# Ordering the weight differences, the residual's turns and its moves between the splits of a decoder layer

## The chip, the cores and the metric

The kernel runs on one core of a Trainium2 chip. A core has five engines that take their instructions in order, each from its own queue: TensorE (PE; its weight loads are listed apart as PEld), VectorE (DVE), ScalarE (ACT), GpSimd (POOL) and SyncE (SP, which here only starts transfers). Sixteen DMA engines carry the transfers. The metric is the device time of one execution in microseconds (us).

## What is computed

One decoder layer over 272 tokens (16 meta tokens and 256 others) of width 2048, all in float32: an attention and pooling mixer, a first layer norm, and a gated feed-forward block with a short convolution, followed by a second layer norm. The change lies in the feed-forward block, of which the reference is

```python
def conv_gated_ffn(h, w_up, conv_w, conv_b, w_down):
    T = h.shape[1]
    z = h @ w_up
    zp = jnp.pad(z, ((0, 0), (CONV_WIDTH - 1, 0), (0, 0)))
    z = sum(zp[:, j:j + T] * conv_w[j] for j in range(CONV_WIDTH)) + conv_b
    a, g = jnp.split(z, 2, axis=-1)
    return (jax.nn.gelu(a) * g) @ w_down
...
    h = layer_norm(ALPHA * h + mix, ln1_g[l], ln1_b[l])
    f = conv_gated_ffn(h, w_up[l], conv_w[l], conv_b[l], w_down[l])
    h = layer_norm(ALPHA * h + f, ln2_g[l], ln2_b[l])
```

`w_up` is 2048 x 11264 (an `a` half and a `g` half of 5632 columns each), `w_down` 5632 x 2048.

## The kernel before

*Weights as a stream.* All weights come as blocks of 128 partitions x 2048 float32 (1 MB) in one fixed order, the list `stream`. A block is landed in a raw tile `wraw`, of which there are three, by a transfer that SyncE starts (L111). It is then split into two float32r parts of less precision, `whl`: ScalarE copies the upper part (L124), VectorE subtracts it from the raw block to get the lower part (L125), in two pieces of 128x1024. A product is then three matmuls: weight upper by activation upper, upper by lower, and lower by upper. A raw tile is free for the transfer three blocks on when its split has been read from it. `weights()` hands out the next block and has blocks up to two further ones recorded ahead of it.

*The feed-forward plan.* The 44 column groups f of the `a` and `g` halves are taken in six parts of 8, 8, 8, 8, 8 and 4 groups (`PARTS`). An *up* item multiplies a block of `w_up` for one f and one half (48 matmuls, L196 to L198, into a PSUM tile `mm`, of which there are four), and its result goes through the convolution `conv` (ScalarE at L715, VectorE at L716 and L717). After the second half `gate` applies the GELU (ACT, L732) and the product (DVE, L733). From the second part on each up item is followed by a *down* item for the part in front, in the function `seven`: it multiplies 256 x 256 x 1024 by seven products in place of eight (Strassen's scheme in Winograd's form). Its A items use four, its B items three of the products (L780 to L782, PSUM tiles `at`). The scheme needs sums and differences of the operands. For the gated activations `forms` makes them on GpSimd (L752 to L755) and splits them (L738 on ACT, L739 on DVE). For the weights they are made in place in the raw tile by VectorE, in `fetch`: one difference in an A block (L116), three operations in a B block (L119 to L121), all 128x512, ahead of the block's split. At the end of four A or B items their products are added to the result `y2` (L788, L792 to L807).

*The residual's way.* The layer's input to the feed-forward block, `y`, lies with channels on the partitions, and `y2` must hold it with tokens on the partitions. It is turned within 32x32 squares by VectorE (L871, one transposition for each of 16 channel groups), and 32 DMA transfers on ScalarE's queue (`residual`, L709; the list `moves`) then carry the squares to their places in `y2`. The part of a move that i numbers is the half of the tokens; all moves of the first half come first.

*What sets the order.* The code is traced, and a scheduler then decides the order in which each engine's instructions stand; they are run in that order. Within `with tc.issue_after(ins)` every instruction traced on the engine of `ins` is ordered behind `ins`. It adds no wait between engines. `behind(i)` uses it with the last upper and the last lower split of block i, which `fetch` returns. The number of the next block to be used is `state["use"]`.

In the up items from f = 4 (`FOLDED`) on, the loop's last lines count them by b = 2 (f - FOLDED) + half. Behind the splits of the next block to be used it records four turns for each b below 4 and, from b = 4 on, four moves, until none is left. These lines stand after the product and its convolution. The first down item comes after b = 8.

Of the kernel before, what the change touches and what calls it, by code (L numbers as in the profile page):

```python
# [14 lines left out]
ALU = mybir.AluOpType  # L15
# [4 lines left out]
NM = 16  # L20
# [4 lines left out]
KT = D // P  # L25
# [11 lines left out]
FOLDED = 4  # L37
# [31 lines left out]
def tile_layer(ctx, tc, xt, w_first, w_proj, w_uk, w_uv, w_pool, w_o, w_up, w_down, cols, rows, rel_bias, onehot, out):  # L69
    nc = tc.nc  # L70
# [7 lines left out]
    def big():  # L78
        return pm.tile([P, 512], F32, tag="mm", name="mm")
# [12 lines left out]
    stream = [w_proj[j] for j in range(8)] + [w_uk, w_uv] + [w_proj[j] for j in range(8, 24)]  # L92
    stream += [w_o[j] for j in range(KT)]
    plan = ffn_plan()
    kinds = {}
# [11 lines left out]
    ready, raws, split = {}, {}, {}  # L107
    state = {"next": 0, "use": 0}

    def fetch(raw, hl, src, kind=None):  # L110
        nc.sync.dma_start(raw, src)  # L111
        b11, b12, b21, b22 = (raw[:, c:c + 512] for c in range(0, 2048, 512))
        cuts = (0, 1024, 2048)
        if kind == "A":

            nc.vector.tensor_tensor(b12, b12, b11, op=ALU.subtract)  # L116
        if kind == "B":

            nc.vector.tensor_tensor(b12, b22, b12, op=ALU.subtract)  # L119
            nc.vector.tensor_tensor(b11, b12, b11, op=ALU.add)  # L120
            nc.vector.tensor_tensor(b21, b21, b11, op=ALU.subtract)  # L121
            cuts = (0, 1024, 1536)
        for c in (slice(a, b) for a, b in zip(cuts, cuts[1:])):
            upper = nc.scalar.activation(hl[:, 0, c], raw[:, c], AF.Copy)  # L124
            lower = nc.vector.tensor_tensor(hl[:, 1, c], raw[:, c], hl[:, 0, c].bitcast(F32), op=ALU.subtract)  # L125
        return upper, lower

    def weight_tiles():
        raw = wp.tile([P, 2048], F32, tag="wraw", name="wraw")
        return raw, wp.tile([P, 2, 2048 + 2], F32R, tag="whl", name="whl")  # L130

    def emit(i):
        if i in ready:
            return
        if i == last:

            raw = wp.tile([P, 2048], F32, tag="wraw", name="wraw")
            nc.sync.dma_start(raw, stream[i])
            raws[i] = raw
            ready[i] = []  # L140
            for c in range(0, 2048, 256):
                hl = ring.tile([P, 2, 258], F32R, tag="act", name="whl_r", padded_shape=[P, 2, T])
                nc.scalar.activation(hl[:, 0, :256], raw[:, c:c + 256], AF.Copy)
                nc.vector.tensor_tensor(hl[:, 1, :256], raw[:, c:c + 256], hl[:, 0, :256].bitcast(F32), op=ALU.subtract)
                ready[i].append(hl)
            return
        if i == spare:
            raw = wp.tile([P, 2048], F32, tag="wraw", name="wraw")
            hl = sb.tile([P, 2, 2048 + 2], F32R, tag="y", name="whl_y")
        else:  # L150
            raw, hl = weight_tiles()
        split[i] = fetch(raw, hl, stream[i], kinds.get(i))
        ready[i] = hl
        if i >= spare:
            raws[i] = raw
# [6 lines left out]
    def weights(ahead=2):  # L162
        i = state["use"]
        state["use"] += 1
        prefetch(i + 1 + ahead)
        return ready.pop(i)

    @contextmanager
    def behind(i):

        upper, lower = (getattr(ins, "ins", ins) for ins in split[i])
        with tc.issue_after(upper), tc.issue_after(lower):
            yield

# [7 lines left out]
    def row_sums(i, hl):  # L182

        total = sb.tile([P, 1], F32, name=f"total{i}")
        nc.scalar.activation(raws[i], raws[i], AF.Copy, accum_out=total)
        hi, lo = (hl[-1][:, p, 256:] if isinstance(hl, list) else hl[:, p, 2048:] for p in range(2))
        nc.scalar.activation(hi, total.to_broadcast([P, 2]), AF.Copy)
        nc.vector.tensor_tensor(lo, total.to_broadcast([P, 2]), hi.bitcast(F32), op=ALU.subtract)
# [16 lines left out]
    for k0, k1 in [(k, k + 1) for k in range(9)] + [(9, 12), (12, 15), (15, 16)]:  # L205
        if k0 == KT - 1:

            raw = ap_.tile([P, 1024], F32, name="wraw_l", tag="v1")[:, :T + MF].rearrange("p (a b) -> p a b", a=1)
        elif k0 % 3 == 0:
            raw = wp.tile([P, 2048], F32, tag="wraw", name="wraw")  # L210
            raw = raw[:, :3 * (T + MF)].rearrange("p (a b) -> p a b", b=T + MF)
        if k0 % 6 == 0:
            hl = wp.tile([P, 2, 2048 + 2], F32R, tag="whl", name="whl")
# [60 lines left out]
    for i in range(2):  # L274
        nc.vector.tensor_tensor(kidx[DI * i:DI * i + DI, 1 + i, :], ps[:DI, :T], kidx[:DI, 0, :].bitcast(F32),
                                op=ALU.subtract)
# [89 lines left out]
    for j in range(8):  # L366
        hl = weights()
# [34 lines left out]
    y = sb.tile([P, KT, T], F32, tag="y", name="x", padded_shape=[P, KT, T])  # L402
# [37 lines left out]
    src = score  # L440
    for r in range(TOPK // 8):
# [4 lines left out]
        src = work  # L446
# [6 lines left out]
    for h in range(H):  # L453
        hl = weights()
# [127 lines left out]
    for h in range(H):  # L582
# [3 lines left out]
        hl = weights()  # L586
# [118 lines left out]
    def residual(a, b, i):  # L705

        src, dst, t = slice(32 * a, 32 * a + 32), slice(32 * b, 32 * b + 32), NM + i * P + 32 * b
        to = y2[dst, i, :].rearrange("p (m d) -> p m d", d=P)[:, :, src]
        nc.scalar.dma_start(to, y[src, :, t:t + 32])  # L709

    moves = [(a, b, i) for i in range(2) for a in range(4) for b in range(4)]

    def conv(j, half_, src, za):
# [98 lines left out]
    for item in plan:  # L812
        if item[0] in "AB":
            seven(*item)
            continue
        if item[0] == "down":
            _, part, c, g = item
            hl = weights()
            if c == 1:
                emit((last, spare)[g])  # L820
                if g == 0:
                    row_sums(last, ready[last])
            if g == 0:
                downs = [big(), big()]
            n = PARTS[part]
            for k in range(4 * g, 4 * g + 4):
                w = slice(512 * (k - 4 * g), 512 * (k - 4 * g) + 512)
                for i in range(2):
                    a, r = pairs[part][k // 2][f"a{i + 1}{k % 2 + 1}"]
                    nc.tensor.matmul(downs[i], a[:, 0, r], hl[:, 0, w], start=k == 0, stop=False)  # L830
                    nc.tensor.matmul(downs[i], a[:, 0, r], hl[:, 1, w], start=False, stop=False)  # L831
                    nc.tensor.matmul(downs[i], a[:, 1, r], hl[:, 0, w], start=False, stop=k == n - 1)  # L832
            if g == n // 4 - 1:
                for i in range(2):
                    yc = y2[:, i, 512 * c:512 * c + 512]
                    nc.vector.tensor_tensor(yc, yc, downs[i], op=ALU.add)
            continue
        _, f, half_ = item
        part = next(p for p in range(len(PARTS)) if f < sum(PARTS[:p + 1]))
        if half_ == 0:  # L840
            if f % 2 == 0:
                pair = fp.tile([P, 2, S], F32, name="za", tag="z0", bufs=3)
            both = []
        hl = weights()
        ps = big()
        if todo and f > FOLDED + half_:
            p, r = todo.pop(0)
            with behind(state["use"]):
                pairs[p].append(forms(r, len(pairs[p]), p == FAST))
        if f < FOLDED:  # L850
            k = 0
            if f + half_ == 0:
                product(ps[:, :NE], hl, P, folded, 0, NE, k1=8)
                deviation()
                k = 8
            product(ps[:, :NE], hl, P, folded, 0, NE, k0=k)
            with behind(state["use"]):
                while len(h_parts) < min(KT, 2 * (2 * f + half_ + 1)):
                    normalise(len(h_parts))
            both.append(ps)  # L860
            if half_ == 0:
                continue
            both = [conv(i * FT + f, i, unfold(both[i]), pair[:, f % 2]) for i in range(2)]
        else:
            product(ps[:, :NQ], hl, P, h_parts, 0, NQ)
            both.append(conv(half_ * FT + f, half_, ps, pair[:, f % 2]))
            with behind(state["use"]):
                b = 2 * (f - FOLDED) + half_
                for m in range(4 * b, 4 * b + 4):
                    if m < KT:  # L870
                        nc.vector.transpose(y[:, m, NM:], y[:, m, NM:])  # L871
                for _ in range(4):
                    if moves and b > 3:
                        residual(*moves.pop(0))
            if half_ == 0:
                continue
        gate(*both)
        if part > FAST:
            a = fp.tile([P, 2, NE], F32R, name="gp", tag="gp", bufs=16)
            gated.append(two_parts(a[:, :, :S], both[0]))  # L880
        elif f % 2:
            todo.append((part, pair))
# [191 lines left out]
```

## Time and profile before

| | |
|---|---|
| median of 3 runs | 1052.95 us (1052.31 to 1056.21) |
| the profiled execution's own time | 1056.32 us |
| its span, first to last instruction | 1054.4 us |
| TensorE busy | 1037.2 us (98% of the span) |
| VectorE, ScalarE, GpSimd busy | 886.7, 623.1, 196.2 us |
| mean granted TensorE clock | 0.994 |
| transfers | 250.28 MB, mean 237 GB/s |

A row of the order of time gives start, duration, engine, line, operation, output from input, shapes, the count, and in square brackets how long the engine was idle before it and what ended that. A row of the waits gives the waiting engine and line, the one it waited for, and the total, number and longest of these waits in us. A row of busy time by stretches gives the stretch and its length, for each engine its busy us and instructions, and last the granted clock as a share of full speed, the busy share of the DMA engines and GB/s. Rows marked SPq or ACTq are the start of a transfer by that queue. Durations of matmuls are modelled and overlap, so distances between starts are used for them.

### The profile page before, as it was taken

To read this page: it belongs to the slowest core of one execution; us is meant where nothing else is said; L and a number is where in the kernel's file an instruction comes from. 1 tells how busy PE (TensorE), PEld (TensorE's weight loads), DVE (VectorE), ACT (ScalarE), POOL (GpSimd) and SP (SyncE) were. 2 spreads that over 40 slices of the span, in tenths; PEclk is the share of its full clock that TensorE was granted. 3 is DMA by queue.
4 is the path that set the end of the run, shared out by engine and by line. 5 is a ranking of instruction groups with operands and counts; after the bars stand their busy time and mean duration, and the time that the engine had idled before them with its cause. 6 is when DMAs were issued, how large, how long until landed. Compare 5 with 4: busy or idle time off the path is not lost.

```text
span 1054.4 us, 19205 instructions
## 1 busy us (share of the span) xinstructions
PE 1037.2 (98%) x7639; PEld 985.2 (93%) x7639; DVE 886.7 (84%) x1401; ACT 623.1 (59%) x1000; POOL 196.2 (19%) x248
## 2 busy tenths in 40 slices
PE   9999999999999999799999999999999999999997
PEld 8999999999999999689999999999999999999986
DVE  6879568758779986689998989989899899989876
ACT  7656456645448755456565565655655656555665
POOL 1200014125430011022122021120211212220031
PEclk9999999999999999899999999999999999999999
DMA  9755543454544567589787887877878778788865
GB/s 322 254 187 220 206 141 131 144 188 164 196 161 165 187 197 221 189 265 313 255 296 279 292 286 248 281 281 270 301 254 282 281 292 269 263 279 274 293 208 162
DMA packets 59754, 250.28 MB, mean 237 GB/s; under 512 B 21734, under 2 KB 22416, under 8 KB 32656
## 3 DMA queue, kind: packets, MB, share of 16 engines
q1 hardware_dynamic: 34592, 230.42, 60.5%
q0 software_dynamic: 7888, 16.14, 8.1%
q10 hardware_dynamic: 17184, 2.49, 1.4%
q8 instruction: 60, 0.98, 0.4%
q14 instruction: 30, 0.25, 0.1%
HBM read 232.50 MB, written 2.11 MB: 222 GB/s over the span
## 4 chain that ended last, share of the span: by engine, by line
PE 82%; DVE 9%; DMA 3%; issue 3%; ACT 2%; POOL 1%; ACTq 0%; SPq 0%; POOLq 0%; DVEq 0%
PE mm L197 19%; PE mm L196 19%; PE mm L198 19%; PE at L781 5%; PE at L782 5%; PE at L780 5%; DVE whl L125 4%; DMA wraw<-in_w_down 2%; PE mm L831 1%; PE mm L832 1%; PE mm L830 1%; ACT whl L124 1%; PE mm L267 1%; DVE hp L702 1%; DMA y<-x 0%
## 5 line engine op out<-in xcount | busy, mean ns | idle before, releaser
L125 DVE TENSOR_TENSOR whl<-wraw,whl 128x1024 fp32r<-128x1024 f32 (+1 forms) x416 | 486.7, 1206 | 38.6 <-ACT whl L124 37.6
L124 ACT ACTIVATE whl<-wraw 128x1024 fp32r<-128x1024 f32 (+1 forms) x416 | 402.5, 1015 | 130.4 <-issue 28.7
L197 PE MATMUL mm<-hp,whl 128*128 128x258 f32 x1280 | 362.7, 283 | 0.7 <-DVE hp L702 0.7
L196 PE MATMUL mm<-hp,whl 128*128 128x258 f32 x1280 | 361.6, 283 | 0.0
L198 PE MATMUL mm<-hp,whl 128*128 128x258 f32 x1280 | 361.3, 282 | 0.0
L197 PEld LDWEIGHTS mm<-hp,whl 128*128 128x128 f32 x1280 | 242.9, 190 | 4.1 <-DVE hp L702 0.9
L196 PEld LDWEIGHTS mm<-hp,whl 128*128 128x128 f32 x1280 | 242.8, 190 | 3.4
L198 PEld LDWEIGHTS mm<-hp,whl 128*128 128x128 f32 x1280 | 242.9, 190 | 0.2
L196 PE MATMUL mm<-xp,whl 128*128 128x256 f32 (+5 forms) x384 | 111.9, 291 | 0.0
L197 PE MATMUL mm<-xp,whl 128*128 128x256 f32 (+5 forms) x384 | 108.7, 283 | 0.0
L198 PE MATMUL mm<-xp,whl 128*128 128x256 f32 (+5 forms) x384 | 108.7, 283 | 0.0
L781 PE MATMUL at<-whl,gp 128*128 128x512 f32 x180 | 73.0, 407 | 6.2 <-DVE whl L125 6.2
L715 ACT ACTIVATE z<-mm,cv 128x256 f32<-128x256 f32 x40 | 22.5, 563 | 89.0 <-PE mm L198 88.9
L196 PEld LDWEIGHTS mm<-xp,whl 128*128 128x128 f32 x384 | 72.4, 189 | 1.0 <-issue 0.5
L197 PEld LDWEIGHTS mm<-xp,whl 128*128 128x128 f32 x384 | 72.3, 188 | 0.4
L198 PEld LDWEIGHTS mm<-xp,whl 128*128 128x128 f32 x384 | 72.4, 189 | 0.3 <-DVE whl L125 0.2
L782 PE MATMUL at<-whl,gp 128*128 128x512 f32 x180 | 72.1, 402 | 0.0
L780 PE MATMUL at<-whl,gp 128*128 128x512 f32 x180 | 69.3, 395 | 0.0
L752 POOL TENSOR_TENSOR forms<-za 128x128 f32<-128x128 f32 x20 | 25.6, 1278 | 209.6 <-DVE za L733 143.8
L755 POOL TENSOR_TENSOR forms<-za 128x128 f32<-128x128 f32 x20 | 23.8, 1190 | 206.2 <-DVE za L733 192.9
L715 ACT ACTIVATE za<-mm,cv 128x256 f32<-128x256 f32 x40 | 22.5, 562 | 66.1 <-PE mm L198 62.7
L781 PEld LDWEIGHTS at<-whl,gp 128*128 128x128 f32 x180 | 34.8, 193 | 14.0 <-DVE whl L125 7.5
(346 smaller groups left out, 1921.1 us busy)
## 6 DMA issues: line engine op xcount, KB each, us to landing
wraw<-in_w_up SPq DMA_DIRECT2D x88, 1024.0 KB, 5.0
wraw<-in_w_down SPq DMA_DIRECT2D x80, 1024.0 KB, 6.4
wraw<-in_w_proj SPq DMA_DIRECT2D x24, 1024.0 KB, 5.0
wraw<-in_w_o SPq DMA_DIRECT2D x16, 1024.0 KB, 4.9
y<-v POOLq DMA_DIRECT2D x27, 256.0 KB, 8.4
y<-u POOLq DMA_DIRECT2D x18, 256.0 KB, 5.0
wraw<-in_w_first SPq DMA_DIRECT2D x8, 304.0 KB, 5.6
x<-in_xt SPq DMA_DIRECT2D x1, 2176.0 KB, 8.8
```

The lines of the kernel that those rows point to most:

```text
L124: upper = nc.scalar.activation(hl[:, 0, c], raw[:, c], AF.Copy)
L125: lower = nc.vector.tensor_tensor(hl[:, 1, c], raw[:, c], hl[:, 0, c].bitcast(F32), op=ALU.subtract)
L196: nc.tensor.matmul(ps, wh, ah, start=n == 0, stop=False)
L197: nc.tensor.matmul(ps, wh, al, start=False, stop=False)
L198: nc.tensor.matmul(ps, wl, ah, start=False, stop=n == KT - 1)
L267: nc.tensor.matmul(ps[:m, :T], wl, x_parts[k][:, 0, :], start=False, stop=k == KT - 1)
L715: nc.scalar.activation(z, src[:, 2:NQ], AF.Identity, bias=col(C_B, j), scale=col(C_W, 3 * j + 2))
L752: nc.gpsimd.tensor_tensor(s[:, 0], a21, a22, op=ALU.add)
L755: nc.gpsimd.tensor_tensor(s[:, 3], a11, a21, op=ALU.subtract)
L780: nc.tensor.matmul(ps, a[:, 0, i], hl[:, 0, w], start=j == 0, stop=False)
L781: nc.tensor.matmul(ps, a[:, 0, i], hl[:, 1, w], start=False, stop=False)
L782: nc.tensor.matmul(ps, a[:, 1, i], hl[:, 0, w], start=False, stop=j == n - 1)
```

## The change

`fetch` gets the last lower split of the block in front in the stream as `front`, and the first difference of an A or a B block is ordered behind it on VectorE. It returns the bare instructions. The turns and moves are taken out of the end of the up item and recorded ahead of its forms, product and convolution. Turns are ordered behind the last lower split of the block after the next one, moves behind its last upper split, each on its own engine. There are 2, 4, 5 and 5 turns for b = 0 to 3; 4 moves for b = 4 to 7, and 3 for each later b until none is left. Since this stands in every up item, b may be negative for f below 4, where nothing is recorded.

```diff
-    def fetch(raw, hl, src, kind=None):
+    def fetch(raw, hl, src, kind, front):
+
         nc.sync.dma_start(raw, src)
         b11, b12, b21, b22 = (raw[:, c:c + 512] for c in range(0, 2048, 512))
         cuts = (0, 1024, 2048)
         if kind == "A":
 
-            nc.vector.tensor_tensor(b12, b12, b11, op=ALU.subtract)
+            with tc.issue_after(front):
+                nc.vector.tensor_tensor(b12, b12, b11, op=ALU.subtract)
         if kind == "B":
 
-            nc.vector.tensor_tensor(b12, b22, b12, op=ALU.subtract)
+            with tc.issue_after(front):
+                nc.vector.tensor_tensor(b12, b22, b12, op=ALU.subtract)
             nc.vector.tensor_tensor(b11, b12, b11, op=ALU.add)
             nc.vector.tensor_tensor(b21, b21, b11, op=ALU.subtract)
...
-        return upper, lower
+        return tuple(getattr(ins, "ins", ins) for ins in (upper, lower))
...
-        split[i] = fetch(raw, hl, stream[i], kinds.get(i))
+        split[i] = fetch(raw, hl, stream[i], kinds.get(i), i and split[i - 1][1])
...
-        upper, lower = (getattr(ins, "ins", ins) for ins in split[i])
+        upper, lower = split[i]
...
+    turns = list(range(KT))
     moves = [(a, b, i) for i in range(2) for a in range(4) for b in range(4)]
...
         hl = weights()
         ps = big()
+
+        b = 2 * (f - FOLDED) + half_
+        upper, lower = split[state["use"] + 1]
+        with tc.issue_after(lower):
+            for m in turns[:(2, 4, 5, 5)[b] if 0 <= b < 4 else 0]:
+                nc.vector.transpose(y[:, m, NM:], y[:, m, NM:])
+                turns.remove(m)
+        with tc.issue_after(upper):
+            for _ in range(0 if b < 4 else 4 if b < 8 else 3):
+                if moves:
+                    residual(*moves.pop(0))
...
             both.append(conv(half_ * FT + f, half_, ps, pair[:, f % 2]))
-            with behind(state["use"]):
-                b = 2 * (f - FOLDED) + half_
-                for m in range(4 * b, 4 * b + 4):
-                    if m < KT:
-                        nc.vector.transpose(y[:, m, NM:], y[:, m, NM:])
-                for _ in range(4):
-                    if moves and b > 3:
-                        residual(*moves.pop(0))
             if half_ == 0:
                 continue
```

## The prediction

> **What bounds the kernel now.** I read the busy shares first, then busy time by stretches, then who waited for whom, and last the order of time around the waits.
>
> ```profile
> PE 1037.2 (98%) x7639; PEld 985.2 (93%) x7639; DVE 886.7 (84%) x1401; ACT 623.1 (59%) x1000; POOL 196.2 (19%) x248
> ...
> 0.00:300.00 300.00, 298.07 (x2389) 290.81 (x2390) 223.88 (x412) 171.75 (x341) 68.58 (x100) 1.00 0.56 195
> ...
> 405.00:465.00 60.00, 52.59 (x348) 47.63 (x347) 42.43 (x60) 28.28 (x41) 12.01 (x10) 0.94 0.72 222
> 465.00:1022.00 557.00, 557.00 (x3908) 522.28 (x3907) 506.31 (x699) 333.37 (x466) 92.38 (x102) 1.00 0.82 278
> 1022.00:1054.40 32.40, 25.66 (x148) 21.51 (x146) 20.74 (x43) 20.86 (x39) 9.96 (x20) 0.92 0.46 146
> ```
>
> A stretch gives its length, then busy us of PE, PEld, DVE, ACT and POOL, the granted clock, the DMA share and GB/s. TensorE is the bound: after 465 us it has no gap at all for 557 us. So no order on another engine can win anything there. Of its 17.2 idle us, 7.4 (60.00 - 52.59) lie in 405 to 465 us, and the clock is below 1.00 there. The built order of instructions differs between the two kernels on DVE and ACT only from about 361 to 475 us of this trace (DVE instructions 518 to 655 of 1387, ACT 402 to 515 of 1004); POOL and SP are the same throughout, PE in two short swaps. The change lives in the one place where PE stands still in mid-run.
>
> ```profile
> PE at L781 <- DVE whl L125: 7.0, 4, 3.3
> ...
> 413.65 0.50 PE L781 MATMUL at<-whl,gp 128*128 128x512 f32 x1 [0.24 <-DVE whl L125]
> ...
> 425.27 0.80 PE L781 MATMUL at<-whl,gp 128*128 128x512 f32 x1 [2.67 <-DVE whl L125]
> ...
> 438.71 0.80 PE L781 MATMUL at<-whl,gp 128*128 128x512 f32 x1 [3.28 <-DVE whl L125]
> ...
> 456.26 0.50 PE L780 MATMUL at<-whl,right 128*128 128x512 f32 x1 [0.45 <-ACT whl L124]
> 457.52 0.50 PE L781 MATMUL at<-whl,right 128*128 128x512 f32 x1 [0.76 <-DVE whl L125]
> ```
>
> Every gap is at a down block (L781), waiting for its lower half (L125). The five sum to 7.40 us, the whole idle time of the stretch. Call the down blocks A0 to A3, B0, B1; an up block U lies between each two. The gaps stand at A1, A2, A3 and B1.
>
> ```profile
> 411.77 0.69 DVE L116 TENSOR_TENSOR wraw<-wraw 128x512 f32<-128x512 f32 x1 [2.00 <-DMA wraw<-in_w_down]
> 412.38 4.62 DVE L125 TENSOR_TENSOR whl<-wraw,whl 128x1024 fp32r<-128x1024 f32 x4
> ...
> 418.02 0.42 DVE L733 TENSOR_TENSOR za<-za,z 128x256 f32<-128x256 f32 x1
> 423.38 0.69 DVE L116 TENSOR_TENSOR wraw<-wraw 128x512 f32<-128x512 f32 x1 [4.94 <-DMA wraw<-in_w_down]
> 423.99 1.22 DVE L125 TENSOR_TENSOR whl<-wraw,whl 128x1024 fp32r<-128x1024 f32 x1
> ...
> 429.05 0.48 DVE L717 SCALAR_TENSOR_TENSOR za<-mm,cv,za 128x256 f32<-128x256 f32 x1
> 436.83 0.69 DVE L119 TENSOR_TENSOR wraw<-wraw 128x512 f32<-128x512 f32 x1 [7.30 <-DMA wraw<-in_w_down]
> 437.44 3.49 DVE L125 TENSOR_TENSOR whl<-wraw,whl 128x1024 fp32r<-128x1024 f32 x3
> ```
>
> This is the cause. With buffer numbers the order reads: at 411.77 the difference of A2, then the splits of A1 and of its U; at 423.38 the difference of A3, then the splits of A2 and U; at 436.83 that of B0, then A3 and U. The difference of a block that is still on its way stands ahead of splits whose data came long ago (A2 landed by 411.77, its split began at 423.99). VectorE idled 2.00, 4.94 and 7.30 us with that work queued behind.
>
> It feeds itself: the three raw buffers come free by those splits.
>
> ```profile
> 414.76 0.33 SPq L111 DMA_DIRECT2D wraw<-in_w_up  x1
> 417.03 0.33 SPq L111 DMA_DIRECT2D wraw<-in_w_down  x1
> ...
> SPq L111 <- DVE whl L125: 156.4, 34, 10.8
> ```
>
> A3's transfer was issued at 417.03, the moment the splits at 412.38 (4.62 long) were through, and the next difference waited for that transfer.
>
> **The change part by part.** *Differences behind the front block's splits (L116, L119).* The new order is split A2, split U, difference A3, and so on. No instruction is added.
>
> ```profile
> 415.54 1.99 ACT L124 ACTIVATE whl<-wraw 128x1024 fp32r<-128x1024 f32 x2
> ...
> 424.65 2.01 ACT L124 ACTIVATE whl<-wraw 128x1024 fp32r<-128x1024 f32 x2 [1.36 <-DVE wraw L116]
> ```
>
> These are the upper halves of A2 and of A3, which a split needs first. At A2: VectorE was free at 418.44 (418.02 + 0.42), ScalarE had the upper halves done at 417.53, and the two splits take 2.35 us (4.62 / 2 a block), so A2 is whole at 420.8; PE asked for it at 422.60 (425.27 - 2.67). At A3: free at 429.53 with the upper halves done at 426.66, whole at 431.9, asked for at 435.43. Both stalls go, with 1.8 and 3.5 us to spare even if nothing before had come earlier. Each earlier split also issues the transfer of the third block after it earlier, so the spare grows from block to block. A1's 0.24 goes likewise: its split stood 2.00 us behind the wait for A2.
>
> What is queued behind the moved wait now: after the difference come the convolutions (L716, L717), the gate and the next splits, all of a block later than it. They wait only if a transfer is late, and it is issued two splits earlier than before.
>
> *B1's 1.21 us.* Before, L120 and L121 of B1 stood behind the four splits of the forms (L739), which wait for GpSimd; now all three differences stand ahead of them.
>
> ```profile
> 453.40 0.55 ACT L715 ACTIVATE za<-mm,cv 128x256 f32<-128x256 f32 x1
> ...
> 455.15 3.48 ACT L124 ACTIVATE whl<-wraw 128x1024 fp32r<-128x1024 f32 x4 [1.20 <-issue]
> ```
>
> ScalarE could go on at 453.95 instead of 455.15: 1.20 us, about the stall. But the rest of this chain (gate, forms on GpSimd, L738, L715) stays, and PE arrives sooner. The bounds are 0 and 1.2 us left, and with its slow chain unmoved up to 3; I leave 0.8.
>
> *Slow clock behind the stalls.*
>
> ```profile
> 422.00:429.00 7.00, 4.33 (x15) 3.29 (x14) 5.62 (x6) 3.30 (x4) 0.00 (x0) 0.76 0.46 105
> 434.00:443.00 9.00, 5.72 (x25) 4.57 (x24) 6.17 (x8) 0.98 (x2) 0.00 (x0) 0.81 0.45 124
> 452.00:460.00 8.00, 6.78 (x46) 5.91 (x46) 6.80 (x11) 5.62 (x10) 2.35 (x3) 1.00 0.67 185
> ```
>
> The two long stalls cost clock too: 7.00 x 0.24 = 1.7 and 9.00 x 0.19 = 1.7 us, at most 3.4; some of it falls into the idle time, so I take 3.2. B1's short stall left the clock at 1.00. The Trainium skill (TensorE: Matmul & The Clock Gate, "What's actually happening") puts the throttle behind an idle window of about 3.4 us. Here 2.67 and 3.28 were enough, so the trace does not agree on the length; by the page the sum would have no clock term and the change would give 3.2 us less.
>
> *Turns and moves.*
>
> ```profile
> L871 DVE STREAM_TRANSPOSE x<-x x16: 398/414/436, 361.5 to 376.7; 128x256 f32<-128x256 f32 x16
> ...
> L709 ACTq DMA_DIRECT2D y<-x x32: 592/640/917, 377.2 to 436.8; - x32
> ...
> DMA to landing us min/median/max: 2.2/2.5/6.4
> ```
>
> ```profile
> 412.32 1.08 PE L780 MATMUL at<-whl,gp 128*128 128x512 f32 x4
> ...
> 421.51 1.09 PE L780 MATMUL at<-whl,gp 128*128 128x512 f32 x4
> ```
>
> The counts stay: 16 turns (6.6 us of VectorE) as 2, 4, 5, 5 in place of 4, 4, 4, 4, in a stretch in which PE has no gap; 32 moves (32 x 0.64 = 20.5 us of ScalarE's queue) as four groups of 4, then of 3. They move from behind the convolution (L715) to behind the next block's upper halves and ahead of the convolution. So those halves come sooner and a convolution up to 4 x 0.64 = 2.6 us later. What covers that: a product goes to one of four PSUM tiles, and A1 to A2 took 8.95 us without the stall (421.51 - 412.32 - 0.24), so PE would have to get more than two such turns ahead. Without the cover it would be about ten groups of 2.6, 26 us. I cost it at nothing. The last moves are issued two up blocks later; the first add into the half of the residual that needs them (L788, with v) is ordered one up block behind the last issue, about 8.9 us against 2.5 to 6.4 for the landing. Nothing on SP or POOL is passed.
>
> **Sum.** 7.4 idle + 3.2 clock - 0.8 left at B1 = 9.8 us. The profiled execution took 1056.32 us (span 1054.4 and 1.9 around it), so 1046.5. The median shown is 1052.95, 3.4 lower. If this difference sits in the stalls (landing times scatter, and a stall too short drops no clock), the changed kernel still comes to 1046.5, for the floor is PE's; if it sits elsewhere, to 1043.1. Outside 405 to 465 most idle time is the 6.7 us of the last 32 us, so I lean to the first: 1045.5.
>
> **The rivals.**
>
> ```profile
> DMA to landing us min/median/max: 4.7/5.3/10.9
> ```
>
> This is the weight blocks' line (L111). *A. One stall comes back* (a late landing, or a convolution behind the moves): about 3 us and 1.7 of clock on top of 1046.5, so 1051, within the measurement. For it: landings reach 10.9 us. Against it: the spare of 1.8 and 3.5 us, which grows.
>
> *B. Transfers bound the stretch, and order only says who waits.* Then 1053. For it: VectorE's idle time is put down to DMA in all three rows. Against it: the DMA share is 0.72 there and 0.82 later at full PE, and both transfers could have been issued sooner.
>
> *C. Slower: GpSimd's forms stretch under a fuller VectorE.* Place: L752 to L755 ahead of B1.
>
> ```profile
> L752 POOL TENSOR_TENSOR forms<-za x20: 461/1102/5791, 359.5 to 935.9; 128x128 f32<-128x128 f32 x20
> ...
> 445.66 5.79 POOL L752 TENSOR_TENSOR forms<-za 128x128 f32<-128x128 f32 x1 [26.61 <-DVE za L733]
> 451.53 0.46 POOL L753 TENSOR_TENSOR forms<-forms,za 128x128 f32<-128x128 f32 x1
> ```
>
> One took 5.79 us against a median of 1.10. If the three that lie in B1's chain all did, B1 would come 2 x 5.3 = 10.6 us late plus 1.7 of clock: 12.3 more than the 9.8 won, so 1059. It decides from about 10 us on. Against it: from 465 us on VectorE is 91% busy (506.31 of 557) and PE never waited for the forms. The Trainium skill (SBUF — State Buffer, "Who interferes with whom") says that a VectorE instruction with two SBUF inputs contends with a GpSimd instruction that reads SBUF; the 5.79 us beside back-to-back tensor_tensor agrees.
>
> **How the numbers follow.** Forecast 0.73, A 0.13, B 0.08, C 0.06. The forecast's bounds are 1043.1 less 0.8 (nothing left at B1), so 1042.3, and 1046.5 with 2 us more left there, 1048.5; reaching to A's half, the range is 1042.5 to 1050.5. 0.5% of 1053 (5.3 us, about what can be told from no change) puts the line at 1047.7. The forecast lies nearly all below it, A and B above: faster 0.76, same 0.17, slower 0.07.
>
> **What would show it.** In 405 to 455 us VectorE's idle time ahead of L118 and L122 (the new L116 and L119) falls below 2 us at a time, or it is idle with no split queued; PE's waits for L125 fall from 7.0 to under 1.5 us; the clock stays at 1.00 there; A2 begins within 1 us of 421. Wrong if PE waits elsewhere in this stretch (for forms, for PSUM, or at the up blocks), or if the gaps at A2 and A3 stay with a transfer as their cause.

## The result and the profile after

The changed kernel takes 1045.54 us (median of 5 runs, 1044.66 to 1045.91). The kernel before, run beside it, took 1056.21 us (5 runs, 1052.31 to 1056.52). The ratio is 0.9909, with a 95% interval of 0.9888 to 0.9930. This median of before is higher than the 1052.95 us shown ahead; three more sets of its runs had medians of 1054.66, 1054.89 and 1055.23 us. The profiled execution took 1045.81 us, with a span of 1044.0 us. Lines of the changed kernel lie a few below: the transfers are L112, the differences L118 (A) and L122 to L124 (B), the splits L127 and L128, the down blocks' matmuls L784 to L786, the adds L792.

First the busy shares of the changed kernel, then its busy time by stretches (columns as before), then, for the kernel before and the changed one, the stretch from the start of A0's product to that of A4, as the first block of the A item behind B0 to B3 is called here. In both kernels this stretch holds the same matmuls.

```profile
PE 1034.6 (99%) x7639; PEld 984.2 (94%) x7639; DVE 888.2 (85%) x1401; ACT 623.2 (60%) x1000; POOL 194.8 (19%) x248
```

```profile
405.00:455.00 50.00, 50.00 (x356) 46.92 (x355) 40.71 (x57) 27.33 (x39) 7.94 (x7) 1.00 0.81 255
...
405.00:465.00 60.00, 59.16 (x416) 55.00 (x415) 50.71 (x69) 33.78 (x47) 7.94 (x7) 1.00 0.79 252
465.00:1022.00 557.00, 557.00 (x3896) 521.65 (x3895) 502.38 (x696) 338.16 (x471) 96.37 (x118) 1.00 0.82 276
```

```profile
403.76:480.94 77.18, 69.78 (x471) 63.80 (x470) 59.12 (x83) 39.44 (x57) 15.70 (x14) 0.96 0.74 240
```

```profile
403.96:471.00 67.04, 66.20 (x470) 61.76 (x469) 57.55 (x80) 38.58 (x54) 10.54 (x12) 1.00 0.80 258
```

TensorE's idle time in 405 to 465 us went from 7.40 to 0.84 us (60.00 - 59.16), and there is none up to 455. The clock there went from 0.94 to 1.00. After 465 us there is still no gap up to 1022. The same matmuls, from A0 to A4, took 77.18 us before and take 67.04 now. These 10.14 us are nearly all of the 10.4 by which the span is shorter: 6.56 us are idle time, and 3.58 are busy time (69.78 to 66.20), which is about what the clock explains (60.00 x 0.06 = 3.6). The other 0.3 us lie ahead of this stretch and in the tail. Over the whole trace TensorE's busy time fell by only 2.6 us, because in the last 32 us its clock was lower in the changed kernel's execution (0.90 against 0.92), where in turn it idled 1.2 us less.

The order of time of VectorE in the changed kernel, around the splits of A1, A2 and A3:

```profile
406.61 4.63 DVE L128 TENSOR_TENSOR whl<-wraw,whl 128x1024 fp32r<-128x1024 f32 x4
411.16 0.68 DVE L118 TENSOR_TENSOR wraw<-wraw 128x512 f32<-128x512 f32 x1
...
414.78 4.89 DVE L128 TENSOR_TENSOR whl<-wraw,whl 128x1024 fp32r<-128x1024 f32 x4
419.60 0.68 DVE L118 TENSOR_TENSOR wraw<-wraw 128x512 f32<-128x512 f32 x1
...
427.70 0.69 DVE L122 TENSOR_TENSOR wraw<-wraw 128x512 f32<-128x512 f32 x1
```

No bracket stands behind the three differences: none of them waited. Before, the differences in these places had waited 2.00, 4.94 and 7.30 us. Each block is now split ahead of the next block's difference. The row at 414.78 holds four splits: two of A2, which end at 417.41, and two of its up block, which end at 419.67 (414.78 + 4.89). Before, A2's split only began at 423.99.

The starts of the transfers on SyncE's queue in the changed kernel:

```profile
417.43 0.33 SPq L112 DMA_DIRECT2D wraw<-in_w_up  x1
419.70 0.33 SPq L112 DMA_DIRECT2D wraw<-in_w_down  x1
```

Each follows the splits that free its raw buffer: the second comes 0.03 us after the splits of 414.78 end. The corresponding pair of before stood at 426.38 and 428.65 us, 9 us later. So transfers come sooner because splits do.

What is left is one stall. It is a row of TensorE's waits, and the chain of waits before it shows why:

```profile
PE at L785 <- DVE whl L128: 0.8, 1, 0.8
```

```profile
446.99 6.80 DMA wraw<-in_w_up
...
453.89 1.07 ACT whl L127
454.96 0.02 issue
454.99 1.84 DVE whl L128 x2
456.82 0.04 issue
456.87 0.50 PE at L785
```

It stands at B2, one block later in the work than the 1.21 us at B1 of before. Its VectorE rows say how:

```profile
452.89 1.22 DVE L128 TENSOR_TENSOR whl<-wraw,whl 128x1024 fp32r<-128x1024 f32 x1
454.99 2.96 DVE L128 TENSOR_TENSOR whl<-wraw,whl 128x1024 fp32r<-128x1024 f32 x3 [0.88 <-ACT whl L127]
```

By buffer numbers the order is B2's first piece, the up block's first piece, B2's second piece, the up block's second. The up block's transfer took 6.80 us, and B2's second piece stood behind the up block's first. It is the same pattern in small: work of a block in front behind work of a block still on its way.

### The profile page after: what moved, and what is told of

It is laid out like the page before. It is cut to its first block, busy times and chain, and to the rows that moved or that the text cites. A ratio compares the mean times of both kernels' runs of the same rounds, so it can differ in the third digit from the quotient of the medians.

```text
span 1044.0 us, 19202 instructions
## 1 busy us (share of the span) xinstructions
PE 1034.6 (99%) x7639; PEld 984.2 (94%) x7639; DVE 888.2 (85%) x1401; ACT 623.2 (60%) x1000; POOL 194.8 (19%) x248
## 4 chain that ended last, share of the span: by engine, by line
PE 85%; DVE 6%; issue 3%; DMA 3%; ACT 2%; POOL 1%; SPq 0%; POOLq 0%; DVEq 0%; ACTq 0%
PE mm L200 21%; PE mm L199 21%; PE mm L201 21%; PE at L785 5%; PE at L784 5%; PE at L786 5%; DVE whl L128 3%; DMA wraw<-in_w_first 1%; DMA wraw<-in_w_down 1%; ACT whl L127 1%; DMA wraw<-in_w_up 1%; DVE hp L705 0%; DVE x L700 0%; DVE x L701 0%; PE at L358 0%
## 5 line engine op out<-in xcount | busy, mean ns | idle before, releaser
L128 DVE TENSOR_TENSOR whl<-wraw,whl 128x1024 fp32r<-128x1024 f32 (+1 forms) x416 | 488.5, 1208 | 39.5 <-ACT whl L127 38.7
L127 ACT ACTIVATE whl<-wraw 128x1024 fp32r<-128x1024 f32 (+1 forms) x416 | 402.9, 1015 | 115.5 <-issue 27.1
L785 PE MATMUL at<-whl,gp 128*128 128x512 f32 x180 | 71.2, 396 | 0.8 <-DVE whl L128 0.8
L786 PE MATMUL at<-whl,gp 128*128 128x512 f32 x180 | 71.0, 395 | 0.0
L784 PE MATMUL at<-whl,gp 128*128 128x512 f32 x180 | 69.4, 395 | 0.0
L759 POOL TENSOR_TENSOR forms<-za 128x128 f32<-128x128 f32 x20 | 23.3, 1167 | 203.5 <-DVE za L737 203.5
L756 POOL TENSOR_TENSOR forms<-za 128x128 f32<-128x128 f32 x20 | 21.2, 1059 | 203.5 <-DVE za L737 139.1
L786 PEld LDWEIGHTS at<-whl,gp 128*128 128x128 f32 x180 | 33.8, 188 | 7.8
```

Source lines behind the costliest of these rows:

```text
L756: nc.gpsimd.tensor_tensor(s[:, 0], a21, a22, op=ALU.add)
L759: nc.gpsimd.tensor_tensor(s[:, 3], a11, a21, op=ALU.subtract)
L784: nc.tensor.matmul(ps, a[:, 0, i], hl[:, 0, w], start=j == 0, stop=False)
L785: nc.tensor.matmul(ps, a[:, 0, i], hl[:, 1, w], start=False, stop=False)
L786: nc.tensor.matmul(ps, a[:, 1, i], hl[:, 0, w], start=False, stop=j == n - 1)
```

## The experiments

*The differences' order alone.* `fetch` as in the change; turns and moves stay where they were. Against the changed kernel:

```diff
-        b = 2 * (f - FOLDED) + half_
-        upper, lower = split[state["use"] + 1]
...
+            with behind(state["use"]):
+                b = 2 * (f - FOLDED) + half_
...
```

> Only the differences are ordered behind the front block's last lower split; turns and moves stay as before. Theory (the order of the differences is the cause): the whole gain, 1045 to 1047 us, ratio to before about 0.991, PE's waits for the down blocks' lower halves under 1.5 us, clock 1.00 from 405 to 455 us. Rival 1 (the moves, out of the way of the upper halves, are the cause): at most a third of the gain, 1052 or more. Rival 2 (both are needed): between, 1048 to 1051.

1046.24 us (4 runs, 1045.97 to 1049.05), ratio 0.9920 (0.9897 to 0.9944). Nearly the whole gain is there without the turns and moves. The profile is of the slowest of the four. It shows one stall (order of time of TensorE, then of VectorE):

```profile
442.36 0.39 PE L201 MATMUL mm<-hp,whl 128*128 128x258 f32 x1 [2.21 <-DVE whl L128]
```

```profile
440.48 0.69 DVE L791 SCALAR_TENSOR_TENSOR y<-y,v 128x512 f32<-128x512 f32 x1 [4.61 <-DMA y<-x]
441.09 2.35 DVE L128 TENSOR_TENSOR whl<-wraw,whl 128x1024 fp32r<-128x1024 f32 x2
```

The add of v into the second half of `y2` waited, and an up block's splits stood behind it. The wait is put down to a move of the residual. In this kernel four of these are started at 429.33 to 432.35 us, just ahead of it. The last of them lands at 440.20 us, 0.28 us ahead of the add. In the changed kernel this add stands at 459.85 us and does not wait.

*Turns and moves alone.* The other half of the change; no difference is ordered. Against the kernel before:

```diff
+        with tc.issue_after(upper):
+            for _ in range(0 if b < 4 else 4 if b < 8 else 3):
+                if moves:
+                    residual(*moves.pop(0))
```

> Only the turns and moves are placed as in the change; no difference is ordered. The built order shows that the scheduler then leaves the differences of A0, A1 and A2 early but puts those of A3 and B0 behind the split in front by itself. Theory: the two long stalls came from the early differences of A3 and B0, so most of the gain is there too, 1046 to 1049 us, with waits of under 2 us left at A1 and A2. Rival 1 (moves are the cause): 1045.5, as with the whole change, and the same in the next kernel. Rival 2 (issue_after alone does it): 1053 to 1056.

1058.11 us (10 runs, 1055.48 to 1058.80), ratio 1.0025 (1.0012 to 1.0038): no gain, and a little loss. TensorE's order of time, then VectorE's:

```profile
417.45 0.80 PE L783 MATMUL at<-whl,gp 128*128 128x512 f32 x1 [2.42 <-DVE whl L126]
458.74 0.80 PE L783 MATMUL at<-whl,right 128*128 128x512 f32 x1 [5.83 <-DVE whl L126]
```

```profile
415.18 0.69 DVE L117 TENSOR_TENSOR wraw<-wraw 128x512 f32<-128x512 f32 x1 [2.64 <-DMA wraw<-in_w_down]
...
456.47 0.69 DVE L120 TENSOR_TENSOR wraw<-wraw 128x512 f32<-128x512 f32 x1 [6.23 <-DMA wraw<-in_w_down]
```

Moving unrelated instructions made the scheduler put some differences behind the front block's splits by itself (A3's and B0's), and others not. Those of A0, A1 and A2 stayed in front, and A1's product now stands for 2.42 us (before 0.24). A new one came in front: the row at 456.47 is B2's difference ahead of B1's splits, and with 5.83 us TensorE's stall at B1 is the longest in this stretch of all the profiles. I had expected 1046 to 1049 us and had not looked for it. So this run does not give the price of the differences of A0 to A2 alone.

*The change with early differences.* As the change, but the differences of A1, A2, A3 and B0 are placed ahead of the lower splits of the block two in front, by an order on VectorE without a wait. No other difference is ordered.

```diff
-            with tc.issue_after(front):
-                nc.vector.tensor_tensor(b12, b12, b11, op=ALU.subtract)
+            firsts.append(nc.vector.tensor_tensor(b12, b12, b11, op=ALU.subtract))
...
+        if kind and 1 < len(firsts) < 6:
+            for ins in lowers[-4:-2]:
+                tc.add_manual_dep(ins, firsts[-1].ins.name, ...)
```

> Turns and moves as in the change, but the differences of A1, A2, A3 and B0 are forced ahead of the lower splits of the block two in front, the order that they had before. Theory: the stalls are back, 1053 to 1057 us, two PE waits of 2 to 3.5 us at A2 and A3 and a clock of about 0.8 around them. Rival 1 (moves): 1045 to 1047. Rival 2 (both): about 1050.

1056.41 us (10 runs, 1053.95 to 1058.78), ratio 1.0011 (0.9996 to 1.0026): the time of before, with the turns and moves of the change. Its VectorE rows, and the row of TensorE's waits:

```profile
415.48 0.69 DVE L118 TENSOR_TENSOR wraw<-wraw 128x512 f32<-128x512 f32 x1 [3.04 <-DMA wraw<-in_w_down]
428.09 0.69 DVE L118 TENSOR_TENSOR wraw<-wraw 128x512 f32<-128x512 f32 x1 [5.53 <-DMA wraw<-in_w_down]
```

```profile
PE at L789 <- DVE whl L131: 6.1, 5, 2.8
```

Where the differences stand decides. Putting them back in front brings back VectorE's waits and the idle time of TensorE.

*The differences left out.* The kernel before without any weight difference of A and B blocks, so its products are those of other operands.

```diff
         if kind == "A":
-            nc.vector.tensor_tensor(b12, b12, b11, op=ALU.subtract)
+            pass
         if kind == "B":
...
-            nc.vector.tensor_tensor(b12, b22, b12, op=ALU.subtract)
-            nc.vector.tensor_tensor(b11, b12, b11, op=ALU.add)
-            nc.vector.tensor_tensor(b21, b21, b11, op=ALU.subtract)
```

> The kernel before with the weight differences of the six down blocks left out (10 VectorE instructions of about 0.6 us, 6 us of work in all); the output therefore differs from the reference. Order and turns and moves are as before. Theory (a difference costs by its wait for a transfer with splits queued behind it, not by its work): the stalls at the down blocks go although nothing is reordered, so 1044 to 1047, PE waits for the lower halves in 405 to 465 us below 1.5 us, clock 1.00 there. Rival (transfers bound the stretch whatever stands in front): 1051 to 1054, with the same PE waits for the lower halves.

1045.91 us (4 runs, 1044.83 to 1046.89), ratio 0.9909 (0.9880 to 0.9938). The count in the expectation is wrong: the edit leaves out 144 instructions, one in each of 36 A blocks and three in each of 36 B blocks, about 99 us of VectorE's instructions (144 x 0.69); VectorE's busy time in the whole trace fell from 886.7 to 801.2 us. Taking all this work away gives no more than ordering it does: it was the wait that cost. This also speaks against the transfers as the bound: with the same three raw buffers and the same 1 MB blocks the stretch ran at a DMA share of 0.93.

```profile
405.00:465.00 60.00, 57.52 (x411) 54.10 (x410) 42.72 (x57) 34.30 (x50) 6.02 (x8) 1.00 0.93 278
```

The 2.48 us that TensorE still stood are at an up block's second piece behind the same add of v, at the same matmul as the 2.21 us of the differences alone.

*One, two and three early.* As the change, with only A3's difference early, or A2's and A3's, or A1's to A3's.

```diff
-            with tc.issue_after(front):
+            with tc.issue_after(split[len(lowers) // 2 - 3][1] if len(firsts) == 4 else front):
...
+            if len(firsts) == 4:
+                for ins in lowers[-4:-2]:
+                    tc.add_manual_dep(ins, first.ins.name, ...)
```

(`in (3, 4)` and `in (2, 3, 4)` in place of `== 4` for the other two.)

> The changed kernel, except that the one difference of A3 stands ahead of the lower halves of A2 and of the up block behind it. Theory (the stall is a feedback: each difference that waits holds the splits that free the raw buffer of a later transfer, so one alone finds its block already landed or nearly so): at most 0.5 us, 1045.5 to 1046.5, VectorE idle less than 2 us ahead of that difference. Rival (each difference that is early costs its own stall): about 3.3 us of idle and 1.7 of clock, 1050 to 1051, with one PE wait of 2 to 4 us at A2.

> The changed kernel, except that the differences of A2 and of A3 stand ahead of the lower halves of the block before each and of its up block (one early: 1046.46). Theory (each wait is handed on through the raw buffers and grows): VectorE waits about 2 us at the first and 5 at the second, TensorE stops 1 to 3 us at A2, 1047.5 to 1050. Rival (each costs the same by itself): not above 1047.5, the second no worse than the one alone.

> The same with the differences of A1, A2 and A3 early. Theory (growing): TensorE stops at A1 or A2 and again at A3, one stall of 2 us or more with a clock below 1.00 behind it, 1050 to 1055, near the kernel with four early (1056.41). Rival (the fourth, B0's, is what makes the stall): 1046 to 1048.

| differences early | us, median | runs | ratio to before | VectorE's waits at A's differences | TensorE's longest stall |
|---|---|---|---|---|---|
| none (the change) | 1045.54 | 1044.66 to 1045.91 | 0.9909 (0.9888 to 0.9930) | none | 0.84 (B2) |
| one | 1046.46 | 1044.55 to 1047.00 | 0.9914 (0.9889 to 0.9939) | 4.58 | 0.85 (B2) |
| two | 1046.22 | 1044.06 to 1049.21 | 0.9922 (0.9896 to 0.9948) | 2.86, 6.07 | 1.67 (A2) |
| three | 1049.82 | 1047.63 to 1052.68 | 0.9952 (0.9928 to 0.9975) | 5.40, 2.50, 4.65 | 2.09 (A2) |
| four (the run above) | 1056.41 | 1053.95 to 1058.78 | 1.0011 (0.9996 to 1.0026) | 4.61 (A0), 6.11, 3.04, 5.53 | 2.82 (A1) |

The waits and stalls are those of one profiled execution each (with two early the slowest of its runs, with three the fastest). The last row is not a pure step of the series: there A0's difference, which nothing orders, stands early too. VectorE's rows with one early, then with two:

```profile
418.64 0.69 DVE L120 TENSOR_TENSOR wraw<-wraw 128x512 f32<-128x512 f32 x1 [4.58 <-DMA wraw<-in_w_down]
```

```profile
409.52 0.69 DVE L120 TENSOR_TENSOR wraw<-wraw 128x512 f32<-128x512 f32 x1 [2.86 <-DMA wraw<-in_w_down]
...
422.66 0.69 DVE L120 TENSOR_TENSOR wraw<-wraw 128x512 f32<-128x512 f32 x1 [6.07 <-DMA wraw<-in_w_down]
```

One alone makes VectorE wait 4.58 us, more than the 2 I had expected, and yet TensorE hardly stops: A2's split still comes in time. With two, the second waits 6.07 us, and the profiled execution (1049.21, the longest of its four) has a stall of 1.67 us at A2. Its median is below what I had given for growth, so two are still mostly absorbed. With three the time is clearly up, close to the 1050 to 1055 us expected, with a clock of 0.83 behind the one stall of its profile. The medians of none, one and two can't be told apart by their intervals. So the spare covers the first waits, and more of them are paid by TensorE. That each wait lengthens the next does not show in these rows: with three and four early the waits do not grow from block to block.

*Every lower split behind the front block's.* The change, and the splits themselves ordered too, which takes the interleave at B2 away.

```diff
-            lower = nc.vector.tensor_tensor(hl[:, 1, c], raw[:, c], hl[:, 0, c].bitcast(F32), op=ALU.subtract)
+            with tc.issue_after(front) if front else ExitStack():
+                lower = nc.vector.tensor_tensor(hl[:, 1, c], raw[:, c], hl[:, 0, c].bitcast(F32), op=ALU.subtract)
```

> The changed kernel, in which the lower splits too are ordered behind the last lower split of the block in front, so that the second piece of B2 no longer stands behind the first piece of the up block after it. Theory: the last stall in mid-run (0.84 us at B2, of which the transfer of that up block was the cause) goes, 1044.3 to 1045.2 us, 0.5 to 1 us less than the changed kernel. Rival: that wait is covered or another takes its place, no change (within 0.3 us) or a loss of up to 2 us where a split now waits that went ahead before.

1045.31 us (4 runs, 1044.01 to 1046.39), ratio 0.9909 (0.9884 to 0.9934). In the profile TensorE's idle time in 405 to 465 us is 0.17 us:

```profile
405.00:465.00 60.00, 59.83 (x426) 56.02 (x425) 50.85 (x69) 33.47 (x46) 8.55 (x7) 1.00 0.78 253
```

So the 0.84 us at B2 do come from the order of the pieces, and can be had. Beside runs that spread over 2 us they can't be measured.

*What turns and moves are worth once the differences are ordered.* The differences alone and the full change, once more, on one chip.

> The differences ordered, turns and moves as before, once more. Theory: 1045.5 to 1046.5 in most executions, with an occasional one some 3 us higher when a move lands late under an add that waits for it; in its profile either no PE wait above 1 us in 405 to 465 us, or one behind an add that waits for a move. Rival (the late add was only that one run's scatter, and the order with moves first has it as often): the same times as the full change, within 0.3 us in the median, with outliers in neither or in both.

> The full change, to be compared on one chip with the differences alone. Theory (turns and moves only keep an add from meeting a late move): median within 0.7 us below that of the differences alone, no execution more than 2 us above its median. Rival (the moves are worth time of their own): 1 us or more below it.

1046.23 us (6 runs, 1044.38 to 1046.54) against 1044.92 us (6 runs, 1044.43 to 1046.06). In this profile of the differences alone, TensorE waits again at the same up block, for 1.1 us:

```profile
PE mm L201 <- DVE whl L128: 1.1, 1, 1.1
```

The three profiles that have moves in their old places and no early difference (these two, and the one with the differences left out) all have this stall (2.21, 1.1 and 2.48 us); three of the full order (the changed kernel twice, and with the splits ordered too) have none there. In two of the three the profile names ScalarE as what ended the add's wait, but in all three the last of the four moves lands 0.27 or 0.28 us ahead of the add: at 440.20, 439.11 and 440.75 us, with the add at 440.48, 439.38 and 441.03. So in each it is a move that the add waits for. The means differ by 0.85 us, with an interval of about -0.1 to 1.8 worked out from the two sets of six. With all 10 runs against all 11, on several chips, it is 1.1 (0.25 to 2.0). So the moves seem to be worth about 1 us, not shown beyond doubt by the times alone. The expectation that the median differs by less than 0.7 fell: by the medians it is 1.31, as the rival's 1 us or more had it; an execution more than 2 us above its median came only in the first set.

*The kernel before, twice more.*

> The kernel before once more, for a second profile. Theory (the 3 to 5 us between its executions, 1052.4 to 1058.8, lie in the stalls at A1 to A3 and B1, which move with landing times): TensorE busy time in 465 to 1022 us the same as in the first profile (557.0 of 557.0), and the difference between the two profiles' spans found within 2 us in 405 to 465 us; a profile of about 1052.5 shows one stall of 2 us or more fewer, or no clock below 1.00. Rival (the executions differ elsewhere, in the load at the start or the tail): the same stalls as in the first profile whatever the time.

> The kernel before, one more profile (those so far are of executions of 1056.32 and 1057.57). If this execution is a short one (1052 to 1053.5), the theory that its stalls set the time says: TensorE idle in 405 to 465 us 2 to 4 us less than the 7.40 and 7.11 there, or its clock there above 0.94; the rival says 7 us of idle and 0.94 again, with the difference elsewhere. If it is a long one, it tells nothing new.

The first took 1057.57 us with a span of 1055.8 (10 runs of it had a median of 1054.61, 1052.84 to 1057.57; ratio to the same kernel 1.0001, 0.9989 to 1.0014), the second 1053.80 us with a span of 1052.0. The stretch of the same matmuls, A0 to A4, in the first:

```profile
404.29:481.52 77.23, 70.12 (x471) 64.40 (x469) 60.45 (x84) 40.34 (x58) 12.78 (x15) 0.96 0.76 246
```

That is 0.05 us more than in the first profile of before (77.18), with stalls of other sizes (0.90, 3.34 and 0.66 us at A1, A2 and A3, and 2.21 us at the up block behind B0, whose splits stood behind B1's difference, which waited 1.50 us). The 1.4 us by which its span is longer lie ahead of this stretch and in the tail, so what sets these two apart is what the rival named, the start and the tail. Stretches of the second, the short one:

```profile
405.00:465.00 60.00, 53.12 (x356) 48.07 (x355) 44.50 (x62) 29.93 (x43) 8.57 (x10) 0.97 0.74 231
420.00:430.00 10.00, 6.75 (x43) 5.63 (x43) 5.64 (x7) 4.47 (x5) 0.00 (x0) 1.00 0.54 151
435.00:445.00 10.00, 7.55 (x42) 6.59 (x41) 9.19 (x13) 3.28 (x6) 0.35 (x1) 0.83 0.70 216
...
403.61:479.05 75.44, 68.56 (x471) 62.76 (x469) 59.46 (x83) 39.78 (x57) 12.23 (x14) 0.98 0.76 245
```

Against the first profile of before (60.00, 52.59, clock 0.94) TensorE's idle time in 405 to 465 us is 0.53 us less and its clock 0.03 more. The same matmuls, A0 to A4, took 75.44 us in place of 77.18: 1.74 of the 2.4 us by which the spans differ, 0.5 of them idle and 1.2 clock. So between these two executions most of the difference sits in the stalls, and most of that is whether a stall costs clock; the rest lies ahead of the stretch and in the tail.

## Why the prediction was right

*What bounds the kernel.* Right. Of the 10.4 us of the span 10.14 lie between A0 and A4, and from 465 to 1022 us TensorE is still without a gap.

*The cause.* Right, and shown: the time goes up again when the differences are put back in front, and it falls just as far when they are left out. That the cost does not go by the number of waits is shown by the series of none to four: one early difference costs VectorE 4.58 us and TensorE hardly anything, four cost all that the change had won. The feedback through the three raw buffers is seen in the starts of the transfers, which come 9 us earlier once the splits do. How much of the cost it makes is not shown: a fixed spare that runs out would give such a series too, and no run has another number of raw buffers.

*The stalls at A1, A2 and A3.* Right: A2 was forecast whole at 420.8 and is at 417.41. It is 3.4 us earlier, since the forecast counted nothing for the splits ahead of it that now come sooner too. Its product begins at 421.03, where within 1 us of 421 was said; this sign tells little, for before it began at 421.51 and stood only after its first four matmuls.

*What was left at B1.* The size (0.8 forecast, 0.84 measured) was right by luck, the place and the cause were not. B1 came in time. The remaining stall is at B2, from a 6.80 us transfer and an order of split pieces that I had not looked at.

*The slow clock.* I had taken 3.2 us of at most 3.4. For the same matmuls, A0 to A4, TensorE's busy time fell by 3.58, so the term was 0.4 too small for this pair of profiles. In any one execution of before it depends on which stalls fell so that the clock dropped: two of them in the first two profiles, one in the short one.

*The sum.* 7.4 + 3.2 - 0.8 = 9.8 against 10.14 measured between A0 and A4: 6.56 idle and 3.58 clock. The other 0.3 of the span is no part of the change's way. The choice between 1046.5 and 1043.1 came out on the side I leaned to: the short execution of before owes most of its time to the stalls, and the changed kernel does not scatter with it (all 11 of its runs lie in 1044.43 to 1046.06). That 1045.5 is the median almost to the digit is luck. It was a lean between two sums that lie 3.4 us apart, and the start and the tail move by 0.7 and 1.3 us between executions of before (1055.8 against 1052.0 in the span).

*Turns and moves at nothing.* This was right for the full change, and incomplete. Alone they gain nothing (1.0025). With the differences ordered they keep an add from standing in front of an up block's splits while it waits, about 1 us. I had looked at this add only for whether the last moves land in time after the change, not at what it did in the order of before. There I had taken a landing of 2.5 to 6.4 us from the kernel before; with the differences ordered and the moves in their old places one took 9.3 us, in the changed kernel up to 7.8.

*The rivals.* No stall came back (A). Transfers did not bind (B): the same stretch carried 252 GB/s in place of 222, and the one without differences 278. The forms did not stretch (C): the first of B1's chain took 1.37 us. The 5.79 us before was that one execution's: in the two later profiles of the kernel before this instruction took 1.98 us, and no run here shows what had stretched it.

## What to carry to other kernels

On an engine that runs its queue in order, work on a block still in transfer that stands ahead of work on a landed one can cost twice, as it did here: by its own wait, and by the buffer that the held work would have freed, which makes the next transfer start late. Look for an idle row ended by a DMA with ready work right behind it, and order the later block's first instruction behind the earlier block's last. An order that a scheduler happens to find is not kept: moving unrelated instructions changed which differences stood in front.

## What was not expected of the hardware

The length of a stall does not say whether TensorE's clock drops after it. The granted clock is that of the stretch of 10 us that holds the time behind the stall:

| kernel | stall, us | clock behind it |
|---|---|---|
| before, short execution | 3.25 | 1.00 |
| differences left out | 2.48 | 1.00 |
| before, short execution | 2.44 | 0.83 |
| differences alone | 2.21 | 0.83 |
| three early | 2.09 | 0.83 |
| four early | 1.84 | 0.83 |
| two early | 1.67 | 1.00 |

The row of the differences alone, and that of the ones left out:

```profile
440.00:450.00 10.00, 7.79 (x51) 7.56 (x50) 9.04 (x15) 3.70 (x5) 0.00 (x0) 0.83 0.63 166
```

```profile
440.00:450.00 10.00, 7.52 (x56) 7.01 (x55) 8.97 (x14) 6.16 (x12) 1.12 (x2) 1.00 0.99 288
```

In these rows a drop costs 10.00 x 0.17 = 1.7 us whatever the stall was, and a stall of 1.7 to 3.3 us may or may not bring one. Of the 14 stalls of 1.5 us or more around this stretch in all the profiles, 11 brought one; none of 1.2 us or less did. Behind the longest, 5.83 us, the clock was 0.66 over 455 to 465 us, twice the loss. In the prediction I had tied the drop to length. The Trainium skill (TensorE: Matmul & The Clock Gate, "What's actually happening") says that the activity window is free-running, so that where work falls in it decides when the clock changes. That agrees with this table: a 3.25 us stall without a drop beside a 2.21 us stall with one. No run here shows the window itself, nor why a stall of 1.84 us is enough.
